# Six output-gate units among the folded Fourier granules, five raw buffers, four folded tiles, one half of a modulation vector summed on TensorE

## The chip, the core and the metric

The kernel runs on one core of one Trainium2 chip. The metric is the device time of one execution in microseconds (us). The kernel before took 2020.89 us, the median of three runs (2016.85, 2020.89 and 2022.59).

## What is computed

One inference step of one layer of a diffusion backbone, all in float32. The tokens are 128 context positions and 256 latent positions, 384 columns `T` once transposed; the model width is 2048, the FFN's hidden width 5632.

```python
mod = silu(cond) @ w_ada + b_ada                  # six vectors of 2048, for context and latent
h = rmsnorm(x, norm_pre_mix) * (1 + sc1) + sh1
# mixer
q, k, v, g, lr_f, lr_b, fo = split(h @ w_in)      # 512, 512, 1024, 1024, 16, 16, 1024 columns
o = gla(q, k, v, lr_f) + flip(gla(flip(q, k, v, lr_b)))   # 4 heads, chunked scans both ways
o = rmsnorm_per_head(o) * gla_out_norm * silu(g)
f = fft2(fo, axes=(positions, channels of a group of 256), norm="ortho").real
g_a, g_b = split(sigmoid(h @ w_gate + b_gate))    # 2 x 2048 columns
merged = g_a * (o @ w_br_gla) + g_b * (f @ w_br_four)
x = x + ga1 * rmsnorm(merged @ w_out)
# channel mixing
h = rmsnorm(x) * (1 + sc2) + sh2
x = x + ga2 * rmsnorm((silu(h @ w_ffn_gate) * (h @ w_ffn_up)) @ w_ffn_down)
```

## The kernel before

**Products.** Activations lie transposed, channels on the 128 partitions, positions along the free axis. Every large product is three matmuls: activations and weights are each split into a rounded part (`hi`) and what is left (`lo`), and hi·hi, hi·lo and lo·hi are summed in PSUM. A weight block is 128 x 1024 float32 (0.52 MB). `load` (line 211) starts its DMA into a `raw` tile of the pool `wp`; `split` lets ACT round it into `whi` (line 257) and DVE subtract into `wlo` (line 258); `take` hands out the oldest pair that is ready; `push` is a `load` and a `split`; `grab` is a `take` and a `push`. There are two `raw` buffers and four each of `whi` and `wlo`. The order of all weight blocks is written down once, in the list `srcs`. All DMAs are issued by one engine's queue, SP. The order of instructions on PE, ACT, DVE and POOL is the order of the program; a scheduler places SP's.

**Stages.** In this order: the head (modulation for the first norm, values and part of the queries), the q and k projections, 32 sigmoid-gate units (`w_gate`, stored to `gates_d` in DRAM) beside which the GLA scans run, then the part that the change touches, then `w_out` with residual and norm, then the FFN (lines named `pgu` and `pdn`). The part in question:

- **Granule loop** (`for n in range(8): for h in range(2)`). A granule is one weight block of the Fourier columns of `w_in`, 256 input channels by four tiles of 128 output channels, taken so that it can be folded: `fold_across` (lines 232 and 233, DVE) turns the block into sums and differences of mirrored channels, ACT copies one column of each to `wq` (line 235), rounds the block, and the low part (line 264) is put on the list `low_due`: it runs only in the next granule's `split`, behind that granule's fold. A granule's matmuls (line 1058) add to four PSUM tiles `pfo` that stay open over all 16 granules; line 1066 adds odd-channel sums into `pfq`, once after every second `n`. The moving operand is `hF`, the activations folded over positions: eight tiles of 128 channels in the memory tagged `B`. The function `ahead` fills them beside the gate units; from `n` = 2 to 5 each iteration replaces two (`over_ends`, `over_parts`: DVE and ACT). `nw` meanwhile loads and splits a small table for one leftover channel (`wr`, `wn`).
- **Tables.** `cd` (line 945, 0.99 MB of cosines and sines) loads at the start of this part; POOL clears `nyq` (line 955) at the same place.
- **`mix_order`.** Eight output-gate units `o0` to `o7` (`proj`, one unit being two weight blocks of `w_in`; then `gcol`: three transposes into `pt`, SiLU on ACT, a product on DVE, a split into `oT`), the last five followed by one or two Fourier columns `b` each; then 16 GLA columns `a`, with the other Fourier columns among them. Beside each `o` unit goes a step of the small DFT (`dft`, into `edT`). A `b` column (`four`) takes one block of `w_br_four`, folds it on DVE, does the last product, adds and subtracts on DVE, multiplies by a gate reloaded from `gates_d` and stores to `four_d`. An `a` column takes one block of `w_br_gla`, multiplies by its gate, adds the `b` column reloaded from `four_d` and goes into `mT` a column later. `gate_of` issues the reloads ahead.

**Modulation beside the rest.** `ada_rest` makes the vectors 2, 3 and 4 of `mod` in six halves. A half is 16 steps: load a 128 x 1024 tile of `w_ada` (`adaw`, two buffers) and multiply and add it into `adacc` with two DVE instructions (line 631 or 633); then eight small matmuls with `selr` sum over the partitions into `pr`, ACT copies, PE transposes twice, DVE adds the bias. The generator is stepped from the other stages at the pace in `rate`: 1.0 in the projections, 1.1 in the gate units, 0 in the granules, 0.35 in `mix_order`, 0.82 in `w_out`.

Of the kernel before, what the change touches and what calls it, by code (L numbers as in the profile page):

```python
# [37 lines left out]
XU = 2  # L38
GD = 256
# [66 lines left out]
def tile_step(ctx: ExitStack, tc: tile.TileContext, a, o):  # L106
# [71 lines left out]
    assert next(fourier, None) is None  # L178
# [24 lines left out]
    raws, ready = [], []  # L203

    def load(raw=None):
# [68 lines left out]
    def push(at=None, eng=DVE, hold=False):  # L274
        load()
# [345 lines left out]

    def ada_rest(todo):
        for m in todo:
            for half in range(2):
                acc = adap.tile([P, 2, 1024], F32, tag="adacc", name="adacc")
                for k in range(KT):
                    w = adap.tile([P, 1024], F32, tag="adaw", name="adaw", bufs=2)
                    SP.dma_start(w, a["w_ada"][m - 2, half, k])
                    for c in range(2):
                        if k == 0:  # L630
                            DVE.tensor_scalar_mul(acc[:, c, :], w, spad[:, k, c : c + 1])
                        else:
                            DVE.scalar_tensor_tensor(  # L633
                                acc[:, c, :], w, spad[:, k, c : c + 1], acc[:, c, :], op0=ALU.mult, op1=ALU.add,
                            )
                    yield
                yield
                pr = pss.tile([P, 256], F32, tag="side", name="pr")
                for c in range(2):
                    for j in range(4):  # L640
                        PE.matmul(
                            pr[32 * j : 32 * j + 32, :], selr[:, 32 * c : 32 * c + 32],
                            acc[:, c, j * 256 : (j + 1) * 256], start=c == 0, stop=c == 1,
                        )
                ev = adap.tile([P, 256], F32, tag="adev", name="adev")
                ACT.copy(ev, pr)
                yield
                pt = pss.tile([P, 2, P], F32, tag="side", name="ptm")
                for b in range(2):
                    PE.transpose(pt[:, b, :], ev[:, b * P : (b + 1) * P], ident)  # L650

                src = pt.rearrange("p b (j r) -> p j b r", r=32)
                mh = mods[:, m, 8 * half : 8 * half + 8, :]
                for c in range(2):
                    DVE.tensor_copy(mh[:, :, c].rearrange("p (j b) -> p j b", b=2), src[:, :, :, c])
                bc = lambda v: v[:, 8 * half : 8 * half + 8].unsqueeze(2).to_broadcast([P, 8, 2])
                DVE.tensor_add(mh, mh, bc(bsc1[:, 1, :] if m == 4 else cols[:, m, :]))
                w1 = {2: 1, 4: 2, 5: 3}.get(m)
                if w1 is not None:
                    DVE.tensor_mul(mh, mh, bc(norms[:, w1, :]))  # L660
# [12 lines left out]
    def over_parts(k, r, x):  # L673

        split_act(*(y[:, k % 8 : k % 8 + 2, :] for y in x), r)
# [10 lines left out]
    ada_gen = ada_rest((2, 3, 4))  # L686
    ada = paced(ada_gen, rate)
    with ExitStack() as s:
# [216 lines left out]
        def ahead():  # L905
            hF.extend(alloc_r("B", "hF"))
            for k in range(0, 8, 2):
# [17 lines left out]
        rate[0] = 1.1  # L925
# [13 lines left out]
    with ExitStack() as s:  # L939
# [9 lines left out]
        cl = actp.tile([P, 6 * pw + HT], F32R, tag="C_lo", name="edT")  # L949
        pairs = [x[:, n * pw : n * pw + 2 * HT] for x, k in ((cl, 6), (d2, 2)) for n in range(k)]  # L950
        eT, dT = pairs[:4], pairs[4:]
        pnr = cl[:, 6 * pw :]
# [11 lines left out]
        def dft():  # L964
# [34 lines left out]
            for h in range(2):  # L999
                for m, dst in enumerate((eT, dT)):  # L1000
# [6 lines left out]
                    if h == 1 and m == 0:  # L1007
                        pn = pss.tile([P, HT], F32, tag="side", name="pn")
                        along(0, pn[0:96], lambda n, r_: nyq[0:r_, n, :])
                        ACT.copy(pnr[0:96], pn[0:96])  # L1010
                        DVE.tensor_sub(pnr[64:96], pn[64:96], pnr[64:96].bitcast(F32))
# [33 lines left out]
        for n in range(8):  # L1045
            for h in range(2):
# [15 lines left out]
                if h and n % 2:  # L1062
                    for x_ in range(2):
                        for k in range(2 * n - 2, 2 * n + 2):
                            q = 32 * (k % 4)
# [902 lines left out]
```

## Time and profile before

| What | Value |
|---|---|
| Median of three runs | 2020.89 us |
| The profiled execution | 2022.91 us |
| Its span, first to last instruction | 2021.1 us |
| Mean granted TensorE clock | 0.986 |
| ACT busy | 913.2 us (45%) |
| HBM read, written | 361.94 MB, 16.78 MB |
| DMA, mean over the span | 188 GB/s |

The profile is one execution of the program. Its page gives busy time by engine (PE matmuls, PEld weight loads, DVE vector, ACT scalar, POOL, SP as the issuer of DMAs), then the span cut in 40 slices with a digit for the busy share in tenths, the granted clock of TensorE in the same digits, and what the DMA engines did. Groups of instructions are listed as line, engine, operation, output and inputs with shape, then a count, busy time, mean duration in ns, idle time ahead of them and what ended it. The other views are answers of the same trace: stretches (start and end, length, then for PE, PEld, DVE, ACT and POOL busy time with the number of instructions in brackets, then granted clock, DMA share and GB/s), waits (the waiting instruction, what released it, total us, how often, the longest), the chain of what ended last in order of time (start, length, instruction), and the instructions of one engine in order (start, span of the row, line, operation, count; in square brackets an idle time ahead of the row and what ended it).

### The profile page before, as it was taken

Reading aid. Unit: us, or ns where it says so; the run is one execution under the profiler, and the core shown is the slowest. Engines: PE = TensorE matmul, PEld = TensorE weight load, DVE = VectorE, ACT = ScalarE, POOL = GpSimd, SP = SyncE. Lnnn points to the kernel's source line nnn. Section 1 sums busy time; section 2 is a strip of 40 time slices with the busy share of each in tenths; the row PEclk is TensorE's granted clock in tenths of the full one; section 3 lists DMA queues with packets and bytes.
Section 4 is the critical chain, followed back from the end, with each engine's and each line's share of the span. In section 5 each row is a group of like instructions: output and inputs, shape, how many; then the busy total and the mean of one; then the engine's idle time right before and its main releaser. Section 6 shows DMA issues by size and latency. Waiting matters only on the chain.

```text
span 2021.1 us, 27652 instructions
## 1 busy us (share of the span) xinstructions
PE 1954.2 (97%) x10582; PEld 1719.4 (85%) x10582; DVE 1673.4 (83%) x2184; ACT 913.2 (45%) x1292; POOL 33.2 (2%) x55
## 2 busy tenths in 40 slices
PE   9999999999769989999999999999999999999998
PEld 6779999989669989999988888888888888888886
DVE  5669898888665889796878988999999889987886
ACT  4233544543225654444645444444434444444445
POOL 0000000000000000000300000000000000000001
PEclk9999999999789999999999999999999999999999
DMA  9978677666423688675526362635455454626244
GB/s 390 380 248 265 221 246 248 224 218 222 138 94 117 208 264 268 204 228 177 198 89 210 120 207 80 212 120 177 130 177 162 128 181 136 194 92 191 74 139 153
DMA packets 200596, 380.53 MB, mean 188 GB/s; under 512 B 14092, under 2 KB 126924, under 8 KB 196112
## 3 DMA queue, kind: packets, MB, share of 16 engines
q1 hardware_dynamic: 199936, 378.51, 56.8%
q8 instruction: 83, 1.36, 0.3%
q14 instruction: 49, 0.40, 0.1%
q10 hardware_dynamic: 528, 0.26, 0.0%
HBM read 361.94 MB, written 16.78 MB: 187 GB/s over the span
## 4 chain that ended last, share of the span: by engine, by line
PE 72%; DVE 12%; DMA 10%; ACT 3%; issue 3%; SPq 0%; POOL 0%; ACTq 0%; DVEq 0%; POOLq 0%
PE pgu L306 29%; PE pdn L306 17%; PE pmm L294 17%; DVE adacc L633 4%; DMA raw<-in_w_in 3%; PE pv L448 3%; DVE wlo L258 2%; DMA raw<-in_w_br_gla 2%; ACT whi L257 1%; PE pgm L431 1%; DMA raw<-in_w_gate 1%; PE pmm L1385 1%; DVE wlo L264 1%; DMA adaw<-in_w_ada 1%; DMA slab<-in_w_ada 1%
## 5 line engine op out<-in xcount | busy, mean ns | idle before, releaser
L294 PE MATMUL pmm<-A_hi,whi 128*128 128x384 f32 x1072 | 362.6, 338 | 0.5 <-ACT A_hi L335 0.5
L294 PE MATMUL pmm<-A_lo,whi 128*128 128x384 f32 x1072 | 359.8, 336 | 1.9 <-DVE A_lo L336 1.9
L294 PE MATMUL pmm<-A_hi,wlo 128*128 128x384 f32 x1072 | 359.7, 336 | 0.0
L1532 ACT CAST whi<-u 128x1024 fp32r<-128x1024 f32 x200 | 210.6, 1053 | 284.3 <-DVE u L1516 86.2
L1532 ACT CAST whi<-raw 128x1024 fp32r<-128x1024 f32 x175 | 184.2, 1053 | 199.3 <-PE pgu L306 69.6
L1543 DVE TENSOR_TENSOR wlo<-u,whi 128x1024 fp32r<-128x1024 f32 x200 | 244.2, 1221 | 32.6 <-ACT whi L1532 18.1
L257 ACT CAST whi<-raw 128x1024 fp32r<-128x1024 f32 x165 | 172.8, 1050 | 185.4 <-DMA raw<-in_w_gate 90.7
L306 PE MATMUL pgu<-whi,A_hi 128*128 128x512 f32 x640 | 250.0, 391 | 0.0
L306 PE MATMUL pgu<-whi,A_lo 128*128 128x512 f32 x640 | 249.3, 389 | 0.0
L258 DVE TENSOR_TENSOR wlo<-raw,whi 128x1024 fp32r<-128x1024 f32 x163 | 198.7, 1221 | 56.3 <-ACT whi L257 55.6
L1543 DVE TENSOR_TENSOR wlo<-raw,whi 128x1024 fp32r<-128x1024 f32 x175 | 213.5, 1220 | 36.5 <-ACT whi L1532 26.3
L633 DVE SCALAR_TENSOR_TENSOR adacc<-adaw,spad,adacc 128x1024 f32<-128x1024 f32 x180 | 222.5, 1280 | 2.9 <-DMA adaw<-in_w_ada 2.7
L294 PEld LDWEIGHTS pmm<-A_hi,whi 128*128 128x128 f32 x1072 | 202.1, 189 | 4.5 <-issue 3.0
L294 PEld LDWEIGHTS pmm<-A_lo,whi 128*128 128x128 f32 x1072 | 202.3, 189 | 2.4 <-DVE A_lo L336 2.2
L294 PEld LDWEIGHTS pmm<-A_hi,wlo 128*128 128x128 f32 x1072 | 202.2, 189 | 0.0
L306 PE MATMUL pdn<-whi,hid_hi 128*128 128x512 f32 x480 | 186.9, 389 | 0.0
L306 PE MATMUL pdn<-whi,hid_lo 128*128 128x512 f32 x480 | 186.8, 389 | 0.0
L306 PE MATMUL pgu<-wlo,A_hi 128*128 128x512 f32 x640 | 184.2, 389 | 0.0
L306 PEld LDWEIGHTS pgu<-whi,A_hi 128*128 128x128 f32 x640 | 120.1, 188 | 26.1 <-issue 0.8
L306 PEld LDWEIGHTS pgu<-wlo,A_hi 128*128 128x128 f32 x640 | 120.1, 188 | 25.4
L306 PEld LDWEIGHTS pgu<-whi,A_lo 128*128 128x128 f32 x640 | 120.2, 188 | 25.0
L306 PE MATMUL pgu<-whi,S 128*128 128x512 f32 x480 | 131.1, 395 | 0.0
(409 smaller groups left out, 2997.1 us busy)
## 6 DMA issues: line engine op xcount, KB each, us to landing
adaw<-in_w_ada SPq DMA_DIRECT2D x96, 512.0 KB
raw<-in_w_d SPq DMA_DIRECT2D x88, 512.0 KB
slab<-in_w_ada SPq DMA_DIRECT2D x32, 1024.0 KB
raw<-in_w_gate SPq DMA_DIRECT2D x64, 512.0 KB
raw<-in_w_g SPq DMA_DIRECT2D x48, 512.0 KB
raw<-in_w_u SPq DMA_DIRECT2D x48, 512.0 KB
raw<-in_w_in SPq DMA_DIRECT2D x44, 512.0 KB
u<-in_w_u SPq DMA_DIRECT2D x40, 512.0 KB
```

What stands on the lines that cost most here:

```text
L257: ACT.copy(hi, raw)
L258: sub = lambda: eng.tensor_sub(lo, raw, hi.bitcast(F32))
L264: low_due.append(lambda: (DVE.tensor_sub(lo, raw, hi.bitcast(F32)), ready.append((hi, lo))))
L294: PE.matmul(dst, w[wi][:, k * n + n0 : k * n + n0 + P], x[xi][:, k0 + k, :], start=first and k == 0 and j == 0, stop=last and k == kts - 1 ...
L306: PE.matmul(dst, stat[x_][m], mov(w[w_], m), start=first and w_ == m == x_ == 0, stop=last and w_ == m == 1,)
L431: PE.matmul(pgv[q : q + 32, :], spad[:, k, :], slab[k // (KT // 2)][:, k % (KT // 2), :], start=k < 4, stop=k >= KT - 4,)
L448: PE.matmul(pv[2 * t + g], hT[x_][:, kb, t * P : (t + 1) * P], w_[:, g * 512 : (g + 1) * 512], start=kb == 0 and j == 0, stop=kb == KT - 1 ...
L633: DVE.scalar_tensor_tensor(acc[:, c, :], w, spad[:, k, c : c + 1], acc[:, c, :], op0=ALU.mult, op1=ALU.add,)
L1385: PE.matmul(hp[u], hw[u][j][:, ((k - 1) % 8) * P : ((k - 1) % 8 + 1) * P], h2[m][:, k - 1, :], start=k == 1 and j == m == 0, stop=k == KT ...
L1532: ACT.copy(hi, src)
L1543: DVE.tensor_sub(lo, src, hi.bitcast(F32))
```

## The change

- `in_order` replaces the two nested loops: granule pairs `f0` to `f7` (`across_n`, both `h` of an `n`) and the first six output-gate units, in the order f0 o0 f1 o1 f2 o2 f3 o3 f4 f5 o4 f6 f7 o5. `srcs` follows it. `oT` is allocated ahead of them, in the memory that `hF` had; an early unit's `pt` comes from the pool of the projections' PSUM tiles instead of the other one.
- `hF` is four tiles instead of eight, in the memory tagged `C_lo`. `ahead` fills the four; later tiles are folded inside `across_n`, the `over_parts` of a pair behind the first half of the next. `edT` is allocated in that memory afterwards (`places`).
- A pool `more` gives three extra `raw3` buffers; with `depth[0]` at 5, `push` loads until five blocks are outstanding. Near the end of `in_order` the depth falls to 2, then back to the old way. Tiles for `mix_order` (gates, `yb`, `fd`, `X`) go to a pool `pm` opened after `more` is closed.
- The odd-channel sums are issued after every `n`, half as many at a time.
- `mix_order` is o6, o7, three `b`, then (`a`, `b`) 13 times, then three `a`.
- The sixth half of the modulation, `(4, 1)`, is taken from `ada_rest`. `ada_gemv` loads the same 16 tiles of `w_ada` and sums them on TensorE: in each of 16 steps, one beside each `a` column, four matmuls of 128 x 32 by 128 x 256 in plain float32 into one PSUM tile. What follows the sum is the same code, now `ada_tail`.
- `rate` becomes 1.0 in the gate units and 0.7 in `w_out`; in `mix_order` nothing is stepped but the DFT and the new sum. Two doubled steps of the GLA generator in the gate units go.

```diff
+EARLY = 6
...
+    in_order = []
+    for i in range(EARLY):
+        in_order += [("f", n) for n in ((i,) if i < 4 else (2 * i - 4, 2 * i - 3))] + [("o", i)]
     across = set()
-    for n in range(8):
-        for h in range(2):
+    for b, n in in_order:
+        if b == "o":
+            srcs += two(a["w_in"], 8 + n)
+        for h in range(2 if b == "f" else 0):
...
-    mix_order = [("o", 0), ("o", 1), ("o", 2)]
-    for i in range(3, 8):
-        mix_order += [("o", i)] + [("b", next(fourier)) for _ in range(1 + (i > 4))]
+    mix_order = [("o", i) for i in range(EARLY, 8)] + [("b", next(fourier)) for _ in range(3)]
     for i in range(KT):
         mix_order.append(("a", i))
-        if i in range(1, 13) and i % 3:
+        if i < KT - 3:
             mix_order.append(("b", next(fourier)))
...
     def load(raw=None):
         n, src = next(srcs, (0, None))
         if src is not None:
-            if raw is None:
+            spare = spare_raws.pop() if raw is None and spare_raws else None
+            if spare:
+                raw = spare.tile([P, G], F32, tag="raw3", name="raw3", bufs=3)
+            elif raw is None:
                 raw = wp.tile([P, G], F32, tag="raw", name="raw", bufs=2)
...
-            raws.append((raw, 1 if n in folded else 2 if n in across else 0))
+            raws.append((raw, 1 if n in folded else 2 if n in across else 0, spare))
...
         if raws:
-            raw, pairs = raws.pop(0)
+            raw, pairs, spare = raws.pop(0)
+            if spare and depth[0] > 2:
+                spare_raws.append(spare)
...
     def push(at=None, eng=DVE, hold=False):
-        load()
+        if not depth[0]:
+            load()
+        while len(raws) < depth[0]:
+            load()
         split(at, eng, hold)
...
+    def ada_gemv(m, half):
+
+        def fetch(k):
+            w = adap.tile([P, 1024], F32, tag="adaw", name="adaw", bufs=2)
+            SP.dma_start(w, a["w_ada"][m - 2, half, k])
+            return w
+
+        w = fetch(0)
+        yield
+        pr = pss.tile([P, 256], F32, tag="side", name="pr")
+        for k in range(KT):
+            following = fetch(k + 1) if k < KT - 1 else None
+            for j in range(4):
+                PE.matmul(
+                    pr[32 * j : 32 * j + 32, :], spad[:, k, :], w[:, j * 256 : (j + 1) * 256],
+                    start=k == 0, stop=k == KT - 1,
+                )
+            w = following
+            yield
+        yield from ada_tail(pr, m, half)
...
-    ada_gen = ada_rest((2, 3, 4))
+    ada_gen = ada_rest([(m, half) for m in (2, 3, 4) for half in range(2)][:5])
...
         def ahead():
-            hF.extend(alloc_r("B", "hF"))
-            for k in range(0, 8, 2):
+            both = actp.tile([P, 2, 4, T], F32R, tag="C_lo", name="hF")
+            hF.extend(both[:, n] for n in range(2))
+            for k in range(0, 4, 2):
...
-            n = 0
             while True:
-                n += 1
-                more = [next(gl, 1) for _ in range(1 + (n in (41, 49)))]
-                if more[-1] is None or next(pre, 1) is not None:
+                if next(gl, 1) is None or next(pre, 1) is not None:
                     next(ada, None)
                 yield
 
         sd = side()
-        rate[0] = 1.1
+        rate[0] = 1.0
...
-        for n in range(8):
+        oT = alloc_r("B", "o")
+        due = []
+
+        def across_n(n):
             for h in range(2):
                 w = take()
                 push()
...
-                            mov = hF[x_][:, kt % 8, :]
+                            mov = hF[x_][:, kt % 4, :]
...
-                if h and n % 2:
-                    for x_ in range(2):
-                        for k in range(2 * n - 2, 2 * n + 2):
...
-                if 2 <= n < 6:
-                    if h == 0:
-                        t, r = (pc.tile([P, 2, T], F32, tag=z, name=z) for z in ("ht", "hr"))
-                        over_ends(2 * n + 4, t, r)
-                    else:
-                        over_parts(2 * n + 4, r, hF)
...
+                if h == 0:
+                    for k, r in due:
+                        over_parts(k, r, hF)
+                    due.clear()
+            for x_ in range(2):
+                for k in range(2 * n, 2 * n + 2):
+                    q = 32 * (k % 4)
+                    PE.matmul(
+                        qb[q : q + 4, :], wq[:, k, :], hF[x_][:, k % 4, 0:HT].bitcast(F32),
+                        start=k < 4 and x_ == 0, stop=k >= KT - 4 and x_ == 1,
+                    )
+            if 2 * n + 4 < KT:
+                t, r = (pc.tile([P, 2, T], F32, tag=z, name=z) for z in ("ht", "hr"))
+                over_ends(2 * n + 4, t, r)
+                due.append((2 * n + 4, r))
+
+        def gcol(p, i):
+            pool, tag = (psm, "mm") if i < EARLY else (pss, "side")
+            pt = pool.tile([P, T], F32, tag=tag, name="pt")
...
+        with ExitStack() as wide:
+            more = wide.enter_context(tc.tile_pool(name="more", bufs=1))
+            spare_raws.extend([more] * 3)
+            depth[0] = 5
+            for at, (b, n) in enumerate(in_order):
+                if b == "o":
+                    proj(psm, hT, lambda p: gcol(p, n))
+                else:
+                    across_n(n)
+                    if n % 2:
+                        next(nw, None)
+                if at == len(in_order) - 4:
+                    depth[0] = 2
+                    spare_raws.clear()
+            depth[0] = 0
+        pm = s.enter_context(tc.tile_pool(name="pm", bufs=1))
...
+        places()
...
-        rate[0] = 0.35
         mT, late = None, []
+        beside = ada_gemv(4, 1)
...
-                step(sd)
+                next(beside, None)
             gate_of()
 
+        for _ in beside:
+            pass
...
-        rate[0] = 0.82
+        rate[0] = 0.7
```

More of the change, by code (lines that the diff above doesn't have):

```diff
@@ L620, in tile_step @@
     adap = ctx.enter_context(tc.tile_pool(name="adap", bufs=1))
-    def ada_rest(todo):
[L623 to L631, printed above, removed]
-                        else:
[L633 to L636, printed above, removed]
-                yield
[L638 to L660, printed above, removed]
@@ new lines, in ada_tail @@
+    def ada_tail(pr, m, half):
+        ev = adap.tile([P, 256], F32, tag="adev", name="adev")
+        ACT.copy(ev, pr)
+        yield
+        pt = pss.tile([P, 2, P], F32, tag="side", name="ptm")
+        for b in range(2):
+            PE.transpose(pt[:, b, :], ev[:, b * P : (b + 1) * P], ident)
+        src = pt.rearrange("p b (j r) -> p j b r", r=32)
+        mh = mods[:, m, 8 * half : 8 * half + 8, :]
+        for c in range(2):
+            DVE.tensor_copy(mh[:, :, c].rearrange("p (j b) -> p j b", b=2), src[:, :, :, c])
+        bc = lambda v: v[:, 8 * half : 8 * half + 8].unsqueeze(2).to_broadcast([P, 8, 2])
+        DVE.tensor_add(mh, mh, bc(bsc1[:, 1, :] if m == 4 else cols[:, m, :]))
+        w1 = {2: 1, 4: 2, 5: 3}.get(m)
+        if w1 is not None:
+            DVE.tensor_mul(mh, mh, bc(norms[:, w1, :]))
@@ L1009, in dft @@
                         along(0, pn[0:96], lambda n, r_: nyq[0:r_, n, :])
[L1010 to L1011 removed]
+                        ACT.copy(pnr[0][0:96], pn[0:96])
+                        DVE.tensor_sub(pnr[0][64:96], pn[64:96], pnr[0][64:96].bitcast(F32))
         def nyq_weights():
@@ L1082, in tile_step @@
+        pm = s.enter_context(tc.tile_pool(name="pm", bufs=1))
+        for g in range(4):
+            X.append(pm.tile([P, T], F32, tag="yb", name="X", bufs=4))
+            ACT.copy(X[g], xb[g])
         for q in range(0, P, 32):
```

78 lines of the change are left out of this document (44 added, 34 removed).

## The prediction

> **What bounds the kernel now.** I read the page first (which engine, and where it pauses), then busy time by stage, the waits of one stage, its chain, and the order of instructions there. The page:
>
> ```profile
> span 2021.1 us, 27652 instructions
> PE 1954.2 (97%) x10582; PEld 1719.4 (85%) x10582; DVE 1673.4 (83%) x2184; ACT 913.2 (45%) x1292; POOL 33.2 (2%) x55
> PE   9999999999769989999999999999999999999998
> PEclk9999999999789999999999999999999999999999
> ```
>
> TensorE (PE) is busy for 97%, so most of the span is its own work. One hole shows: slices 11 and 12, where both its busy share and its granted clock fall. That is where the diff works. Cut at the first granule matmul (509.48), the first output-gate matmul (608.61) and the first matmul with `w_out` (811.82), the view of stretches gives two stages (busy us, then clock, DMA share and GB/s at the end):
>
> ```profile
> 509.48:608.61 99.13, 69.84 (x450) 63.62 (x449) 60.60 (x83) 27.17 (x45) 2.31 (x4) 0.78 0.37 118
> 608.61:811.82 203.21, 192.58 (x1153) 186.54 (x1150) 164.20 (x283) 106.14 (x177) 0.00 (x0) 0.99 0.67 217
> ```
>
> Stage A (the 16 Fourier granules): PE idles 29.3 of 99.1 us and runs at 0.78 of its clock. Stage B (8 output-gate units, the small DFT, 16 Fourier and 16 GLA columns): PE idles 10.6 of 203.2. The waits of A and one turn of the chain through it:
>
> ```profile
> PE pfo L1058 <- DVE wlo L264: 29.3, 14, 4.5
> DVE raw L232 <- DMA raw<-in_w_in: 28.6, 12, 4.1
> ```
> ```profile
> 531.73 3.54 DMA raw<-in_w_in
> 535.36 0.70 DVE raw L232
> 536.12 0.57 issue
> 536.70 1.23 DVE wlo L264
> 537.94 3.44 DMA raw<-in_w_in
> ```
>
> PE waits for the low parts, DVE for the load. The turn is 537.94 − 531.73 = 6.2 us: load 3.5, fold 1.3, then the low part of the granule before, whose end frees the buffer for the next load. With two buffers and low parts lagging by a granule, one load is in flight: 16 × 6.2 = 99. It is latency, since the stage moves only 118 GB/s.
>
> **What the pieces cost PE at full clock.** From the order of PE's instructions, start to start:
>
> ```profile
> 511.45 1.14 PE L1058 MATMUL pfo<-hF_hi,wlo 128*128 128x194 f32 x8
> 512.42 0.61 PE L1058 MATMUL pfo<-hF_hi,whi 128*128 128x194 f32 x4
> 512.87 0.61 PE L1058 MATMUL pfo<-hF_lo,whi 128*128 128x194 f32 x4
> 513.32 0.61 PE L1058 MATMUL pfo<-hF_hi,whi 128*128 128x194 f32 x4
> 513.76 0.61 PE L1058 MATMUL pfo<-hF_lo,whi 128*128 128x194 f32 x4
> ...
> 550.05 2.02 PE L1058 MATMUL pfo<-hF_hi,wlo 128*128 128x194 f32 x8 [0.53 <-DVE wlo L264]
> 551.87 1.05 PE L1058 MATMUL pfo<-hF_hi,whi 128*128 128x194 f32 x4
> ...
> 582.96 0.51 PE L1066 MATMUL pfq<-hF_hi,wq 128*4 128x194 f32 x8
> ...
> 583.73 0.69 PE L1058 MATMUL pfo<-hF_hi,whi 128*128 128x194 f32 x4
> ```
>
> A granule is 0.97 + 4 × 0.445 = 2.75 us; at half clock the same eight matmuls take 1.82. The odd-channel sums cost 0.77 four times, 3.1 in all, before and after (the change issues half as many twice as often). So A holds 16 × 2.75 + 3.1 = 47.1 us of work and loses 52: 29 idle, the rest half clock. Output gate (between two transposes), Fourier column, GLA column, and four small matmuls of the kind the change adds:
>
> ```profile
> 647.65 0.49 PE L1111 MATMUL pt<-ident,qk 128*128 128x128 f32 x3
> ...
> 656.31 0.49 PE L1111 MATMUL pt<-ident,qk 128*128 128x128 f32 x3
> 656.55 0.42 PE L1127 MATMUL pf<-edT,whi 128*128 128x388 f32 x1
> ...
> 659.02 0.36 PE L294 MATMUL pmm<-A_hi,whi 128*128 128x384 f32 x1
> ...
> 726.23 0.36 PE L294 MATMUL pmm<-o_hi,whi 128*128 128x384 f32 x1
> ...
> 730.44 0.34 PE L1127 MATMUL pf<-edT,whi 128*128 128x388 f32 x1
> ```
> ```profile
> 99.76 0.61 PE L431 MATMUL pgm<-slab,spad 128*32 128x256 f32 x8
> 100.30 1.66 PE L448 MATMUL pv<-whi,A_hi 128*128 128x512 f32 x6
> ```
>
> 8.66, 2.47 and 4.21 us; 0.54 for four (each recorded twice).
>
> **Stage A after.** Six output-gate units move in: 47.1 + 6 × 8.66 = 99.1 us of PE work, what the stage takes today without them. Five raw buffers let a load start four granules ahead: with at least 4 × 2.75 = 11 us to land in, the 3.5 us of latency goes. Next late is DVE: its 60.6 us, plus six units at two subtractions of 1.22 (row below) and about 1.2 for the gate column, 22, comes to 83 of 99. Its tightest stretch is two folded pairs ahead of one unit: 4 × 2.5 + 2 × 3.3 + 3.6 = 20 us (the 3.3 an estimate from the 60.6: less 16 × 2.5, ada and table work, over five tiles) against PE's 4 × 2.75 + 0.8 + 8.66 = 20.4. It fits, and four split pairs stand ready. Four folded tiles instead of eight cost nothing: each is rewritten a granule pair after its last read.
>
> One new wait stands at the entrance. In the changed kernel's DMA queue the second half of the first output-gate unit goes to a new buffer, behind the cosine tables `cd` (0.99 MB); its first half does not. `cd` waits for a memset, which waits for the gate stage's last accumulation:
>
> ```profile
> POOL nyq L955 <- DVE adacc L633: 132.4, 1, 132.4
> ```
> ```profile
> 517.75 4.87 DVE L633 SCALAR_TENSOR_TENSOR adacc<-adaw,spad,adacc 128x1024 f32<-128x1024 f32 x4
> ```
> ```profile
> 522.41 0.33 SPq L945 DMA_DIRECT2D cd<-in_consts  x1
> ```
> ```profile
> L257 ACT CAST whi<-raw 128x1024 fp32r<-128x1024 f32 x165 | 172.8, 1050 | 185.4 <-DMA raw<-in_w_gate 90.7
> L258 DVE TENSOR_TENSOR wlo<-raw,whi 128x1024 fp32r<-128x1024 f32 x163 | 198.7, 1221 | 56.3 <-ACT whi L257 55.6
> ```
>
> Now this accumulation runs after one granule more; I put its end, and the issue, at 518.5–519. At about 320 GB/s (below) `cd` takes 3.1, the load 1.6 and 1.9 of latency (3.5 − 1.6), cast and low part 2.3: 527.8. PE gets there at 509.5 + 5.9 + 4.2 = 519.6, or 520.3 with a slip of 0.7 for the second granule's low part. Wait 7.5, and a stretch at half clock, 2.5: 10 us. Bounds: 0 (issue at 511) and 16 (issue at 522.4 as now). The four-buffer rings of split weights hide none of it. SP's other loads queue behind `cd` too, but PE asks for them later than this one.
>
> **Stage B after.** Six units leave: 192.6 − 6 × 8.66 = 140.6 us of PE work. The TensorE half of the modulation adds 16 × 0.54 = 8.6: 149.2. It removes 32 DVE instructions:
>
> ```profile
> 767.32 2.48 DVE L633 SCALAR_TENSOR_TENSOR adacc<-adaw,spad,adacc 128x1024 f32<-128x1024 f32 x2
> ```
>
> 16 × 2.4 = 38 us of DVE, 11 steps of it from this stage, which is why DVE no longer holds PE here although it loses the six units as cover: a pair of columns costs DVE 6.9 (from 767 to 787 three GLA columns, two Fourier columns and one such step fill it, 19.35 us), PE 4.21 + 2.47 + 0.54 = 7.22. The other half of the removed steps ran beside PE-bound work and is worth nothing. The 8 small sums of the sixth half, 1.0 us of PE, go from the `w_out` stage.
>
> What comes next in a pair is the loads. Each of 13 pairs moves three weight blocks of 0.52 MB (Fourier, GLA, modulation) and four planes of 0.197 (two gates, store, reload): 2.36 MB in 7.22 us, 327 GB/s. What the queue gives with these transfers:
>
> ```profile
> 720.00:730.00 10.00, 8.98 (x55) 8.65 (x54) 9.37 (x18) 4.72 (x7) 0.00 (x0) 1.00 0.96 333
> 740.00:760.00 20.00, 17.62 (x95) 16.69 (x95) 18.53 (x34) 9.36 (x17) 0.00 (x0) 0.91 0.82 263
> ```
>
> Rate over share is 347 and 321; at 320 and a share of 0.96 a pair takes 7.7 us; 13 × 0.46 = 6.0 more. The ends: 7.22 (PE's pace) and 9.0 (263 GB/s). Entering and leaving add 3.5: `xT` (1.6 MB) loads beside the first Fourier columns, and the last small sum's transposes wait for a copy. B: 149.2 + 9.5 = 158.7.
>
> Waits of 0.5 us per pair should leave the clock alone. But stretches have dropped it for less than the entrance's wait:
>
> ```profile
> 752.42 0.45 PE L1127 MATMUL pf<-edT,whi 128*128 128x388 f32 x1 [1.32 <-ACT whi L257]
> 753.68 0.36 PE L1128 MATMUL pf<-edT,wlo 128*128 128x194 f32 x1 [0.81 <-DVE wlo L258]
> ```
>
> After 2.1 us of idle in two parts the clock of that window is 0.91. The Trainium skill (TensorE: Matmul & The Clock Gate, What's actually happening) halves the clock only after an idle window of about 3.4 us; by that the pairs keep full clock in every case, while by this row two waits close together can cost 1.7 us (half of 3.4). The trace differs from the rule here; the sum is the same by both, only its upper end is not.
>
> **Sum.** Before 99.1 + 203.2 = 302.3. After 109.1 + 158.7 = 267.8. Less 34.5, and 1.0 in the `w_out` stage: 35.5. The profiled execution took 2022.9 (span 2021.1), 2.0 above the median of 2020.9; from the median that is **1985 us**.
>
> **Rivals.** (1) Transfers keep up: pairs at 7.22 and the entrance covered, 35.5 + 10 + 6, some 1970. For: 333 GB/s in the fullest window; against: 0.82 in the others. The Trainium skill (DMA: Bandwidth & Descriptors, Specifications) puts the HBM limit of a core near 358 GB/s; by it a pair's loads take an estimated 6.6 us and PE sets the pace, the same as this rival. No mixed window of this stage reaches it.
> (2) The queue stays at 263 GB/s, since each buffer's load waits for its reader: 9.0 a pair, 13 × 1.3 = 17 more: 2002. For: that is today's rate; against: today DVE paces it.
> (3) Slower: in the pairs, without output-gate units between them, the loads fall to the mean rate of B, 217 GB/s (row above): 10.9 a pair, 13 × 3.2 = 42 more, 2027. It decides from 7.7 + 35.5 / 13 = 10.4 us a pair, 227 GB/s. Against it: B's low mean comes from PE-bound units that ask for little.
> (4) The buffers don't do what they are for, the lagging low part still serialising loads: granules at 6.2, A = 16 × 6.2 + 52 = 151 and no entrance wait: 42 worse, 2027. Against: in the changed queue a load waits only for its own buffer's last reader, and five buffers rotate.
>
> **Numbers.** Forecast 0.50, (1) 0.18, (2) 0.18, (3) 0.05, (4) 0.05, between (2) and no change 0.04. 0.3% is 6 us, about what a measurement of this kernel can tell. Faster 0.86, same 0.04, slower 0.10. The range runs from (1) with B's small additions gone, 1966, to (2) with the entrance's upper end, 2008, and leaves out (3), (4) and a little more.
>
> **What would show it.** Right: PE's waits for low parts in the granules gone but for one of 5 to 10 us ahead of the first output gate's second half, clock near 1 after it, stage A near 109; pairs at 7.5 to 8 us with DMA share above 0.9 and DVE below it. Wrong: waits of 3 us ahead of each granule (4); pairs over 9 us with PE waiting for casts that wait for loads (2, 3), or at 7.2 with idle queues (1); or a `w_out` stage that begins with a longer stall than now.

## The result, and the profile after

The changed kernel takes 1972.9 us (median of four runs, 1972.7 to 1975.3) against 2021.7 for the kernel before (median of four): the ratio is 0.977, 95% interval 0.975 to 0.978. The forecast was 1985, range 1966 to 2008. It is faster by 48.8 where 35.5 were forecast. The page of its profiled execution (1973.01 us):

```profile
span 1971.2 us, 27823 instructions
PE 1940.7 (98%) x10694; PEld 1701.8 (86%) x10694; DVE 1636.9 (83%) x2152; ACT 899.4 (46%) x1282; POOL 33.3 (2%) x55
PE   9999999999999997999999999999999999999998
PEclk9999999999999998999999999999999999999999
```

The hole in slices 11 and 12 is closed; a small one is new, in slice 16. The stretches of the changed kernel (columns as before), cut at its first granule matmul (497.89), the first matmul of o6 (608.52) and the first with `w_out` (768.57), with the gate units ahead of them and ten column pairs (664.02 to 738.26) by themselves:

```profile
200.00:497.89 297.89, 297.34 (x1931) 292.28 (x1931) 253.96 (x333) 145.61 (x249) 1.86 (x6) 1.00 0.72 231
497.89:608.52 110.63, 105.43 (x755) 99.58 (x755) 81.19 (x108) 45.87 (x70) 2.31 (x4) 0.97 0.52 166
608.52:768.57 160.05, 149.94 (x975) 135.75 (x974) 124.32 (x247) 77.60 (x150) 0.00 (x0) 0.97 0.80 263
664.02:738.26 74.24, 74.15 (x492) 67.16 (x491) 67.95 (x139) 35.26 (x66) 0.00 (x0) 1.00 0.92 305
768.57:1971.20 1202.63, 1192.90 (x5696) 1019.80 (x5694) 1038.81 (x1213) 560.65 (x697) 26.71 (x33) 1.00 0.49 155
```

The same view of the kernel before, ahead of and behind the two stages of the prediction:

```profile
200.00:509.48 309.48, 299.69 (x1933) 292.98 (x1933) 264.06 (x345) 145.53 (x249) 1.87 (x6) 1.00 0.70 228
811.82:2021.10 1209.28, 1196.98 (x5713) 1022.10 (x5712) 1047.17 (x1225) 564.77 (x703) 26.65 (x33) 1.00 0.49 157
```

| Part of the span | Before | Forecast | Measured |
|---|---|---|---|
| up to the first granule | 509.5 | no change | 497.9 (−11.6) |
| A | 99.1 | 109.1 | 110.6 |
| B | 203.2 | 158.7 | 160.05 |
| from `w_out` on | 1209.3 | −1.0 | 1202.6 (−6.65) |

A and B together came out 2.9 us from the forecast (270.7 against 267.8). What was missed lies outside them: 11.6 us in the gate units, 5.65 from `w_out` on.

**Gate units.** The waits of PE up to 520 us, of the kernel before:

```profile
PE bT L766 <- ACT lah L335: 3.0, 3, 2.3
PE dl L721 <- DVE part L336: 2.3, 2, 1.5
PE bT L766 <- DVE lal L336: 2.0, 3, 0.7
PE at L806 <- DVE ki L783: 1.3, 1, 1.3
```

These are the GLA chains beside the gate units, and none of them is left in the changed kernel. In the stretches DVE does 12 instructions less there (345 to 333), 10.1 us of work.

**The entrance of A.** The waits of the changed kernel up to 520 us, then PE's order and SP's order there:

```profile
PE pmm L306 <- ACT whi L266: 3.9, 1, 3.9
```
```profile
512.44 0.69 PE L306 MATMUL pmm<-A_hi,whi 128*128 128x384 f32 x1 [3.90 <-ACT whi L266]
...
517.96 0.34 PE L306 MATMUL pmm<-A_hi,whi 128*128 128x384 f32 x1
```
```profile
501.38 0.87 SPq L218 DMA_DIRECT2D raw<-in_w_in  x2
502.96 0.33 SPq L978 DMA_DIRECT2D cd<-in_consts  x1
503.34 1.50 SPq L218 DMA_DIRECT2D raw<-in_w_in  x3
```

The wait ahead of the first unit's second half is there, 4.2 us (3.9, and 0.3 for the low part behind it) instead of the forecast 7.5, and the matmuls behind it run at half clock for 5.3 us. That block is the first of the three at 503.34; two blocks that PE needs later and `cd` go ahead of it.

**The end of B.** The waits of PE from 600 to 830 us; then PE's order, SP's order and SP's wait there:

```profile
PE pr L689 <- DMA adaw<-in_w_ada: 9.0, 3, 6.8
```
```profile
764.13 1.08 PE L689 MATMUL pr<-adaw,spad 128*32 128x256 f32 x8 [6.75 <-DMA adaw<-in_w_ada]
```
```profile
748.39 0.64 SPq L1247 DMA_DIRECT2D Clo<-in_xT  x1
749.12 0.45 SPq L1166 DMA_DIRECT2D yb<-four_d  x1
749.94 0.33 SPq L1197 DMA_DIRECT2D four_d<-y  x1
750.32 0.60 SPq L1247 DMA_DIRECT2D Clo<-in_xT  x1
757.19 0.32 SPq L1166 DMA_DIRECT2D yb<-four_d  x1
757.61 0.38 SPq L218 DMA_DIRECT2D raw<-in_w_out  x1
758.08 0.38 SPq L680 DMA_DIRECT2D adaw<-in_w_ada  x1
```
```profile
SPq L1166 <- DMA four_d<-y: 6.2, 1, 6.2
```

SP reloads the last Fourier column and waits 6.2 us until its store has landed, which was issued next to the loads of `xT`; the tile of `w_ada` that the sum on PE needs next is queued on SP behind that reload, at 758.08.

### The profile page after: what moved, and what is told of

It is laid out like the page before. It is cut to its first block, busy times and chain, and to the rows that moved or that the text cites. A ratio compares the mean times of both kernels' runs of the same rounds, so it can differ in the third digit from the quotient of the medians.

```text
span 1971.2 us, 27823 instructions
## 1 busy us (share of the span) xinstructions
PE 1940.7 (98%) x10694; PEld 1701.8 (86%) x10694; DVE 1636.9 (83%) x2152; ACT 899.4 (46%) x1282; POOL 33.3 (2%) x55
## 4 chain that ended last, share of the span: by engine, by line
PE 67%; DVE 3%; DMA 2%; ACT 1%; issue 1%; SPq 0%; POOL 0%; ACTq 0%; DVEq 0%; POOLq 0%
PE pgu L318 30%; PE pdn L318 17%; PE pmm L306 14%; PE pfo L1098 1%; PE pf L1183 1%; PE pmm L1443 1%; DMA raw<-in_w_br_gla 1%; PE ptr L1735 1%; PE pf L1184 0%; DMA adaw<-in_w_ada 0%; DMA raw<-in_w_d 0%; ACT whi L266 0%; DMA four_d<-y 0%; DVE x1b L1887 0%; PE pr L689 0%
## 5 line engine op out<-in xcount | busy, mean ns | idle before, releaser
L662 DVE SCALAR_TENSOR_TENSOR adacc<-adaw,spad,adacc 128x1024 f32<-128x1024 f32 x150 | 185.7, 1279 | 1.4 <-DMA adaw<-in_w_ada 1.0
```

The lines of the kernel that those rows point to most:

```text
L662: DVE.scalar_tensor_tensor(acc[:, c, :], w, spad[:, k, c : c + 1], acc[:, c, :], op0=ALU.mult, op1=ALU.add,)
```

## The experiments

Beside them the kernel before took 2020.1 to 2020.9 us (medians).

**1. Does the wait for `w_ada` stand in for the old stall at `w_out`?** In the kernel before, the `w_out` stage began with 2.4 us of idle and some 3.4 lost to half clock (a granted clock of 0.66 over 10 us); in the changed one it does not. `gemv_early` begins the sum three steps earlier:

```diff
                 four(i)
+                if i < 3:
+                    next(beside, None)
```

> The changed kernel, with the TensorE sum of the last modulation half begun three steps earlier: one step beside each of the first three Fourier columns as well, so that its last step comes ahead of the last GLA columns. Theory 1 (the two waits of 6.75 and 1.45 us for the last `w_ada` tiles cover a stall at the start of the `w_out` stage that the kernel before had and the changed one does not: 2.4 us idle and 3.4 of half clock): the 9 us of waits and 2.5 of half clock go, and 5.8 come back at the first `w_out` unit; 5 to 6 us faster, about 1967. Theory 2 (the two have nothing to do with each other): all 11.5 us go, about 1961.5. Theory 3 (DMA is what the end of the stage lacks, the tile only the one that shows it): the wait moves to the last `w_br_gla` or the first `w_out` blocks and the time stays within 2 us of 1972.9.

1960.8 us (1960.3 to 1962.5), 12.1 less than the changed kernel. Its stretches for B and behind it:

```profile
608.34:756.42 148.08, 148.08 (x976) 135.56 (x973) 121.62 (x243) 75.42 (x147) 0.00 (x0) 1.00 0.80 273
756.42:1958.50 1202.08, 1192.28 (x5697) 1018.87 (x5695) 1040.50 (x1217) 562.44 (x699) 26.67 (x33) 1.00 0.50 157
```

Theory 2: B falls by 12.0 to 148.1, PE idles not at all, and nothing comes back behind it. The two stalls are separate; theory 1, that one covers the other, fell.

**2. The gate units and the TensorE sum.** Four kernels with the new order and buffers, the sixth half on DVE or TensorE, the pacing of the gate units old or new (`gate_pace_back`, `half_on_dve`, `order_only`, and the changed kernel):

```diff
 gate_pace_back
...
+                n += 1
+                more = [next(gl, 1) for _ in range(1 + (n in (41, 49)))]
...
-        rate[0] = 1.0
+        rate[0] = 1.1
 half_on_dve
-    ... for half in range(2)][:5])
+    ... for half in range(2)])
...
+        rate[0] = 0.5
...
-        beside = ada_gemv(4, 1)
...
-                next(beside, None)
+                step(sd)
...
-        rate[0] = 0.7
+        rate[0] = 0.82
 order_only: both
```

> The changed kernel, with the pace of the modulation sums in the gate units back at 1.1 and the two doubled steps of the GLA generator back. The first granule matmul came at 509.5 us before and comes at 497.9 in the changed kernel, 11.6 that the prediction did not have. Theory 1 (pace and doubled steps are the whole of it: PE waited 8.6 us for DVE and ACT in the GLA chains): the first granule is back at 507 to 510, and the time 10 to 12 us longer, about 1984. Theory 2 (it comes from folding four tiles ahead instead of eight, which leaves DVE and ACT free at the end of the gate units): the first granule stays at 498 to 500, and the time within 2 us of 1972.9.

> The changed kernel, with the sixth half of the modulation back on DVE (16 steps of two multiply-accumulates, stepped at 0.5 beside the last two output-gate units and the GLA columns, and at 0.82 in the `w_out` stage). Theory 1 (the TensorE sum is worth something because DVE would hold the pairs of columns: 6.9 us of DVE a pair, and 1.2 more for half a step, against 7.38 on PE now): pairs of 7.8 to 8.2 us, 13 x 0.6 = 8 us more, less the 11.5 us that the waits for the last `w_ada` tiles cost, and 5.8 more at the start of the `w_out` stage: about 1975, and the `w_out` stage some us longer for its steps. Theory 2 (DVE has room here): pairs of 6.7 to 6.9 us on PE alone, 13 x 0.6 = 8 us less: about 1960.

> The changed kernel, with the sixth half of the modulation back on DVE (at 0.5 in `mix_order`, 0.82 in the `w_out` stage) and the gate units' pacing back at 1.1 with the two doubled steps; what is left of the change is the order, the buffers and the folded tiles. Theory 1 (the gate units' 12 us are paid for by the TensorE sum: with it gone, DVE has to do its 16 steps somewhere, and whichever stage they are taken from passes them on): the first granule at 507 to 510 again, the end of the `w_out` stage shorter than with the half on DVE at the slower pace (1982.95) by about as much: 1979 to 1986. Theory 2 (they add): 1982.95 and 12.4 more, 1995.

And the new pacing alone in the kernel before:

> The kernel before, with only the gate units' pacing of the changed kernel (modulation steps at 1.0 instead of 1.1, no doubled steps of the GLA generator); all six halves stay on DVE. Theory 1 (the 11.6 us of the gate units are an edit of their own): the first granule at 497 to 500 instead of 509.5. The five or six modulation steps that are then left over, 2.5 us of DVE each, fall to the end of the `w_out` stage, where DVE is full, and cost up to 13 us there: the time between 2008 (they find room) and 2022 (they do not). Theory 2 (the gate units gain only together with the other edits, four folded tiles and the shorter list of halves): the first granule after 505.

| Kernel | Half on | Pacing | us | First granule | A and B | From `w_out` on |
|---|---|---|---|---|---|---|
| `order_only` | DVE | old | 1984.9 | 508.6 | 272.0 | 1202.65 |
| `half_on_dve` | DVE | new | 1982.95 | 497.65 | 266.15 | 1218.7 |
| `gate_pace_back` | TensorE | old | 1985.3 | 506.7 | 272.1 | 1203.0 |
| changed | TensorE | new | 1972.9 | 497.9 | 270.7 | 1202.6 |
| before | DVE | old | 2020.1 | 509.5 | 302.3 | 1209.3 |
| `before_gate_pace` | DVE | new | 2024.45 | 497.4 | 303.2 | 1219.9 |

Neither edit is worth more than 2 us alone (1984.9 becomes 1982.95 with the pacing, 1985.3 with the sum); together they take 12. The pacing always brings the first granule forward by 9 to 12 us, and PE's waits in the GLA chains, 6.1 us in `gate_pace_back`, are gone with it; its two parts, the rate and the doubled steps, were not tried apart. With six halves on DVE the steps that were put off come back at the end of the `w_out` stage. The wait of PE there in `half_on_dve` (in `before_gate_pace` it is 6.8 us):

```profile
PE pr L670 <- DVE adacc L662: 7.5, 1, 7.5
```

The TensorE sum takes 32 of these DVE instructions away, and so pays for the pacing. Without the pacing its own costs (8.6 us of PE, and the wait for the last tiles) eat what it saves in B: A and B together take 272.0 us without the sum and 272.1 with it. What it can save is seen in `half_on_dve`, where PE waits 15.2 us for DVE in B (as much in `order_only`):

```profile
PE pmm L306 <- DVE fd L1188: 9.8, 6, 1.8
PE pf L1184 <- DVE wlo L267: 5.4, 10, 0.7
```

`half_on_dve` missed both of its expectations: it lies 8 us above theory 1, which put the `w_out` stage at 5.8 us more for its start and "some us" for the extra steps, where it is 16 us longer. Another spread of its DVE steps was not tried. `before_gate_pace` lies a little above its range, for the same reason. Theory 1 of `gate_pace_back` held in time, with the first granule a little ahead of its 507 to 510. Theory 1 of `order_only` held; it also says that order, buffers and folded tiles alone are worth 35.9 us (1984.9 against 2020.9).

**3. Order or buffers?** `depth_two` keeps the order without the spare buffers, `granules_first` the buffers with all granules ahead of the units.

```diff
 depth_two
-            more = wide.enter_context(tc.tile_pool(name="more", bufs=1))
-            spare_raws.extend([more] * 3)
-            depth[0] = 5
+            depth[0] = 2
 granules_first
-    for i in range(EARLY):
-        in_order += [("f", n) for n in ((i,) if i < 4 else (2 * i - 4, 2 * i - 3))] + [("o", i)]
+    in_order = [("f", n) for n in range(8)] + [("o", i) for i in range(EARLY)]
```

> The changed kernel with its order, but without the three extra raw buffers (two blocks outstanding). Theory 1 (the granule's turn of 6.2 us, load then fold then the low part that frees the buffer, goes on behind the output-gate units, so that a group of one pair and one unit takes 2 x 6.2 + 2 x 2.9 = 18.2 us against 14.9 on PE, a group of two pairs 30.6): stage A 125 to 135 us instead of 101.9, the time 1996 to 2006. Theory 2 (the order alone does it, the loads catch up behind each unit): stage A within 5 us of 101.9, the time 1973 to 1978.

> The changed kernel with its buffers, but all eight granule pairs ahead of the six output-gate units. Theory 1 (with loads far ahead the granules are paced by DVE, 16 x 2.5 of folds and low parts and 6 x 3.3 for the moving tiles, 60 us against 47 on PE): granules and six units in 112 to 122 us instead of 101.9, the time 1983 to 1993. Theory 2 (the buffers are all that is needed): within 3 us of 1972.9. Theory 3 (the lagging low part holds the buffers whatever their number): granules at 6.2 us, 151 us for the two, the time above 2015.

1988.9 and 1995.6. Their stretches, A of `depth_two`, then granules and the units behind them of `granules_first`:

```profile
498.14:626.88 128.74, 111.36 (x756) 104.15 (x755) 82.18 (x108) 46.08 (x70) 2.31 (x4) 0.92 0.44 141
```
```profile
498.60:582.20 83.60, 60.77 (x450) 54.84 (x449) 61.74 (x87) 29.14 (x47) 2.30 (x4) 0.84 0.50 155
582.20:633.90 51.70, 51.70 (x305) 51.53 (x304) 20.14 (x22) 17.38 (x22) 0.00 (x0) 1.00 0.35 103
```

Without the buffers A takes 128.7 us, within the 125 to 135 of theory 1, though the total is below its range. Both expectations start from an A of 101.9 us, which ends at the sixth unit's first matmul (599.82), while their sums hold all six units; counted from 110.6, theory 1 of `depth_two` gives 1987 to 1997, and 1988.9 lies in it. Without the order A takes 135.3, where theory 1 had 112 to 122; the granules fall from 6.2 us to 5.2, so rival 4 of the prediction (6.2 with any number of buffers) is out. The miss has two parts. The waits of `granules_first`:

```profile
PE pfo L1097 <- DVE wlo L272: 12.7, 1, 12.7
PE pfo L1097 <- ACT hF L346: 8.9, 5, 3.5
```

A granule's low part stands behind the fold of a late block at the entrance, and the moving tiles, folded only a pair ahead, come late where no unit covers them. From 99 + 52 = 151 us the order alone takes 22, the buffers alone 16, and both 40: neither does the work of the other, and the two gains nearly add.

**4. The entrance.** `cd_late` issues `cd` after the third entry of the order; `near_buffers` puts the first two early loads into the two old buffers, which are free sooner; `two_pairs_first` is `cd_late` and `gemv_early` with f0 f1 ahead of o0.

```diff
 cd_late
-        SP.dma_start(cd, a["consts"][:, C_CE:NC])
...
+                if at == 3:
+                    SP.dma_start(cd, a["consts"][:, C_CE:NC])
 near_buffers (plain starts at 2)
+            near = raw is None and plain[0] > 0
+            plain[0] -= near
-            spare = spare_raws.pop() if raw is None and spare_raws else None
+            spare = spare_raws.pop() if raw is None and spare_raws and not near else None
```

> The changed kernel, with the load of the cosine tables `cd` issued after the third entry of the order (f0 o0 f1) instead of ahead of it. Theory 1 (the wait of 3.9 us ahead of the second half of the first output-gate unit is that block's load, issued at 503.34 and landing 7.9 us later because the 0.99 MB of `cd` go ahead of it in the same queue): the load lands 3 us earlier and the cast is ready as PE gets there; the wait falls below 1 us, the half clock behind it goes too, and stage A falls from 101.9 to 95.5 us; about 1967. Theory 2 (the block is late because its spare buffer comes free only with the end of the gate units, and five blocks are asked for at once): the wait stays at 3 us or more and the time within 2 us of the changed kernel's 1972.9.

> The changed kernel, with the first two of the five early loads (the second block of the first output-gate unit and the next granule) going to the two old raw buffers, and the later three to the spare ones. Theory 1 (the unit's second block came late because its spare buffer was free only after the last gate column was stored, so that two blocks needed later and `cd` went ahead of it in the queue): it lands at about 505 us, no wait of over 1 us ahead of the second half of the first unit, 6 us less with the half clock; about 1967. Theory 2 (five blocks at once are too much for the queue here, and another block is late in its place): a wait of 2 us or more at one of the next granules or units, 1970 to 1973.

> The changed kernel with three edits: the load of `cd` after the third entry of the order, the TensorE sum of the last half begun three steps earlier, and the order f0 f1 o0 f2 o1 f3 o2 f4 o3 f5 o4 f6 f7 o5, so that PE asks for the first output-gate unit 5.5 us later. Theory 1 (the waits at the two ends are separate, and the first unit's second block is late by 1.9 us for lack of lead alone): no wait of over 1 us in stage A, 96 us there, 157 in stage B; 1972.9 less 12 for the sum and 6 to 7 for the entrance, about 1954. Theory 2 (DVE is short in the first two pairs, which have no unit beside them, as at the end of the loop): PE waits 2 to 5 us for low parts or folded tiles ahead of the first unit, and the time is 1957 to 1960.

`cd_late` takes 1968.25 us; its wait falls from 3.9 to 1.9, less than theory 1 had. `near_buffers` takes 1964.5, with no wait at the entrance and A at 103.6:

```profile
497.88:601.50 103.62, 102.57 (x756) 97.56 (x755) 81.09 (x108) 45.80 (x70) 2.31 (x4) 1.00 0.56 176
```

So `cd` and the two later blocks each delay the block, and the whole entrance costs 7.0 us (110.6 less 103.6). The rest of what `near_buffers` gains lies in B, 157.2 us, where PE waits 7.5 us for `w_ada` instead of 9.0. `two_pairs_first` missed: 1964.1, 3.3 more than `gemv_early` alone. It is theory 2's wait, but 9.5 us long where that had 2 to 5: PE waits there for a granule's low part, which DVE holds behind the fold of a block that has not landed, as in `granules_first`:

```profile
515.65 2.02 PE L1099 MATMUL pfo<-hF,wlo 128*128 128x194 f32 x8 [9.51 <-DVE wlo L275]
```
```profile
513.04 0.69 DVE L241 TENSOR_TENSOR raw<-raw 128x512 f32<-128x512 f32 x1 [8.57 <-DMA raw<-in_w_in]
```

**5. The odd-channel sums**, `four_quarters`:

```diff
-                    q = 32 * (k % 4)
+                    q = 32 * (2 * x_ + k % 2)
...
-                        start=k < 4 and x_ == 0, stop=k >= KT - 4 and x_ == 1,
+                        start=k < 2, stop=k >= KT - 2,
```

> The changed kernel with the odd-channel sums spread over four column groups of PE at a time instead of two: the group is chosen by the part (hi, lo) and the tile instead of by the tile alone; the number of matmuls is the same. Before, eight of these small matmuls on four groups took 0.77 us; in the changed kernel four on two groups take 0.75, eight times in all, 6.0 instead of 3.1. Theory 1 (matmuls on different column groups run side by side, and the change halved how many do): 0.39 us for four, 2.9 us less in all, about 1970. Theory 2 (the 0.75 is a fixed cost of changing to these matmuls and back): no change, 1972.9.

PE's order at the first sums, of the changed kernel and of `four_quarters`:

```profile
503.33 0.83 PE L1109 MATMUL pfq<-hF,wq 128*4 128x194 f32 x8
504.08 0.44 PE L306 MATMUL pmm<-A_hi,whi 128*128 128x384 f32 x1
```
```profile
503.14 0.51 PE L1109 MATMUL pfq<-hF,wq 128*4 128x194 f32 x8
503.58 0.44 PE L306 MATMUL pmm<-A_hi,whi 128*128 128x384 f32 x1
```

0.44 us instead of 0.75 for the same four matmuls, so theory 1 is right on the cause. The Trainium skill (TensorE: Matmul & The Clock Gate, Part 3: Packing small matmuls — row/col tiling) has matmuls on different column tiles run at the same time; the trace agrees, with a factor of 1.7 for twice as many groups. But the time does not move (1972.3): A takes 111.0 us, not less, and PE's wait for the folded tiles near its end grows from 0.75 to 1.6. That wait uses up the gain: the sums save 2.5 us, PE idles 0.9 more, and behind the wait the granted clock is 0.83 over 10 us (587 to 597), where it is 1.00 in the changed kernel, which is another 1.7.

**6. Together**, `all_four`: `cd_late`, `gemv_early`, `near_buffers` and `four_quarters`.

> The changed kernel with four edits: `cd` later in the queue, the TensorE sum begun three steps earlier, the odd-channel sums on four column groups, the first two early loads in the old raw buffers. Theory 1 (four separate losses): 1972.9 less 12.1 for the sum, 6.5 for the entrance and 2.9 for the odd channels: 1951. Theory 2 (at the entrance the low part that lags by a granule takes the place of the late block): 1954 to 1957.

1955.6 us (1954.4 to 1955.7), ratio to the kernel before 0.968 (0.9665 to 0.969): 17.3 faster than the changed kernel, and short of the 1951 of theory 1.

```profile
496.88:601.90 105.02, 103.09 (x756) 99.15 (x755) 81.18 (x108) 45.80 (x70) 2.32 (x4) 0.97 0.54 174
601.90:750.01 148.11, 148.11 (x975) 135.59 (x974) 121.51 (x243) 75.55 (x147) 0.00 (x0) 1.00 0.80 273
```

B has no idle left. A is 1.4 us longer than in `near_buffers` alone, though the odd-channel sums take less; the low part is not what takes the place of the block, so theory 2 has the size but not the cause. What does is the wait for the folded tiles near the end of the loop, and half clock behind it. PE's order there in `all_four`, and the second of these rows in `near_buffers`:

```profile
583.69 0.73 PE L1099 MATMUL pfo<-hF,whi 128*128 128x194 f32 x4 [1.67 <-ACT hF L349]
584.68 2.87 PE L1099 MATMUL pfo<-hF,whi 128*128 128x194 f32 x12 [0.26 <-DVE hF L350]
```
```profile
586.96 1.58 PE L1100 MATMUL pfo<-hF,whi 128*128 128x194 f32 x12 [0.30 <-DVE hF L350]
```

The same twelve matmuls take 2.87 us instead of 1.58, and the granted clock is 0.75 from 586 to 596; in `near_buffers` the first wait is 0.74 and the clock stays at 1.00.

## Why the prediction was right, and where it was not

- **Granules.** Right. PE's waits for their low parts are gone, and it took the buffers and the order both (experiment 3). Of the other side, rival 4 did not come.
- **The entrance.** Right in place and kind, 7.0 us instead of 10. The step on its cause failed: `cd` was to wait for the gate stage's last accumulation and be issued 9 us after the first granule. In the changed kernel the memset ahead of it waits for the store of the last gate column, and `cd` goes out 5.1 us after the first granule (502.96). That two later blocks also overtake the needed one was not seen. POOL's wait ahead of the memset in the changed kernel, and PE's wait at the entrance in `gate_pace_back`:

```profile
POOL nyq L992 <- DMA gates_d<-gz: 119.5, 1, 119.5
```
```profile
526.15 0.69 PE L306 MATMUL pmm<-A_hi,whi 128*128 128x384 f32 x1 [7.42 <-ACT whi L266]
```

With the old pacing `cd` goes out 11.2 us after the first granule and the wait is 7.4 us, about as forecast: the pacing, which the prediction left out, shortened this wait too.

- **Odd-channel sums, "3.1 in all, before and after"**: wrong. They take 6.0 (eight times 0.75), because half as many column groups work at a time. **"Four folded tiles cost nothing"**: wrong by a wait of 1.05 us near the end of the loop, and of 1.9 with half clock behind it where PE is faster (experiments 5 and 6). A's sum: 99.1 of work, 2.9 for the odd channels, 5.2 idle, which leaves 3.4 for half clock and small change.
- **Pairs.** The step that the queue paces them at 7.7 us failed; rival 1's mechanism came instead. Ten pairs took 74.24 us, 7.42 each, with PE idle for 0.1 and the DMA share at 0.92: the queue moved 305 GB/s and had room. PE's own 7.22 was short by 0.2.
- **The end of B.** Without the waits for the last `w_ada` tiles B is 148.1 (experiment 1): the forecast's 149.2 of PE work, and nothing of the 9.5 added to it for pairs and ends. The waits and their half clock, 12 us, were not forecast. That B agreed to 1.4 us comes of two errors that cancel, not of steps that were right.
- **"The other half of the removed steps ... is worth nothing"**: this is the step that failed by most. The edit of the pacing in the gate units stood in the diff and got no term. There PE waited for the GLA chains behind DVE, 9.8 us idle in the stretch before, and DVE steps taken out of one stage make room in another: 11.6 us, of which 2 at most are left without the TensorE sum; and the sum is worth nothing without the pacing (experiment 2). The trace of the kernel before has 20 such DVE instructions in B, ten steps and not 11. `gate_pace_back` comes close to the kernel that the prediction priced, and took 1985.3 us against 1985, but by terms that cancel: A is 115.6 instead of 109.1, and the part from `w_out` on 5.3 us below its forecast. That 1972.9 lies in the range is in part luck: its low side was made for rival 1, and the pacing had no part in it.
- **From `w_out` on**: 6.65 instead of 1.0. By the traces the old stall came from DVE's order. In the kernel before, and in `gemv_early` after it:

```profile
820.55 1.23 DVE L258 TENSOR_TENSOR wlo<-raw,whi 128x1024 fp32r<-128x1024 f32 x1 [4.88 <-ACT whi L257]
821.69 0.55 DVE L1165 TENSOR_TENSOR gate<-gate,pmm 128x384 f32<-128x384 f32 x1
```
```profile
760.72 1.23 DVE L267 TENSOR_TENSOR wlo<-raw,whi 128x1024 fp32r<-128x1024 f32 x1 [4.85 <-ACT whi L266]
```

The last GLA column's product stands behind the low part of a `w_out` block that comes 8.7 us after the stage's first matmul (811.82) there, and 4.3 after it (756.42) here, in time for PE. Why that block comes sooner was not tested.

The clock was half after the 3.9 us wait (512.44 to 517.96), as the Trainium skill (TensorE: Matmul & The Clock Gate, What's actually happening) has it for an idle window of about 3.4 us. Shorter waits did the same, and there the trace differs from that rule: 1.67 and 0.26 us in `all_four` (experiment 6), and in the kernel before 0.51 and 1.93 us at the start of the `w_out` stage, with matmuls at half rate until 829.3:

```profile
823.35 0.69 PE L294 MATMUL pmm<-A_lo,whi 128*128 128x384 f32 x1 [1.93 <-DVE A_lo L336]
```

In `cd_late` 1.87 and 0.65 us at the entrance did not: the clock of its stage A is 1.00. So the sum of two close waits does not decide it, and what does is not shown. The pairs, with PE idle for 0.1 us, test neither the rule nor the row of the prediction.

## What to carry to other kernels

An engine that paces nothing in the stage at hand may pace another: where a change takes steps from DVE, look in the chain of each stage for what DVE holds up, and cost every edit of a pace in the diff, however small. Ask of each early load which queue it stands in and what overtakes it: a block in a buffer that is free later goes out behind blocks that are needed later. An agreement of two totals proves the steps only if the terms agree too.

## What was not expected of the hardware

Four small matmuls of four output channels each took 0.75 us on two column groups of PE and 0.44 on four. The mixed queue of weights, gates and stores held 305 GB/s over 74 us at a share of 0.92, where the fullest 10 us of stage B in the kernel before had shown 333 and 20 us of it 263. A store of 0.2 MB issued between two loads of 0.79 MB held its reader's queue for 6.2 us. Two waits of 1.67 and 0.26 us were followed by about 8 us of half clock, two of 1.87 and 0.65 us by none.
